# Later activations in the gate pairs, and the index keys' chain and scores behind the operand sums, in a hybrid attention and retention block

## The chip, the cores and the metric

The kernel runs on 1 core of one Trainium2 chip. The time is device microseconds of one execution; a time of the kernel is the median of several. The names in the profile: PE multiplies matrices, PEld loads its weights, DVE and ACT work on vectors (ACT with activation functions), POOL is GpSimd, SP issues DMAs. ACT and POOL issue DMAs as well.

## The reference

One layer over 512 tokens of width 2048. The normed input is multiplied by a wide matrix, whose columns feed a sparse attention (an indexer scores keys, the best 128 are taken), a retention over chunks, and two gates:

```python
h = rmsnorm(x, norm_gain)
proj = h @ w_in
(aq, ak, av, az, iq, ik, iw, rq, rk, rv, rz, ga, gb) = jnp.split(proj, SPLIT_POINTS, axis=-1)
iq = iq.reshape(B, L, IDX_HEADS, IDX_DIM) * (IDX_DIM ** -0.5)
ik = plain_layernorm(ik)
...
a_out = dsa_mixer(aq, ak, av, iq, ik, iw, positions, rel_bias) * jax.nn.silu(az)
b_out = retention_mixer(rq, rk, rv, ret_gn_gain) * jax.nn.silu(rz)
merged = jax.nn.sigmoid(ga) * (a_out @ w_a_out) + jax.nn.sigmoid(gb) * (b_out @ w_b_out)
r = x + merged @ w_o
return r + (p_i @ w_ple) * jax.nn.sigmoid(r @ w_ple_gate)
```

The indexer's score is a sum over 16 heads of `relu(iq . ik) * iw`. A last RMSNorm follows the layer.

## The kernel before

**Numbers as two halves.** Every matrix operand is held as a high and a low 16-bit part, and a product is three matmuls: high by high, high by low, low by high. A unit of weights is a raw tile of 32-bit numbers, loaded by SP (L250), of which ACT makes the high part (`high_part`, L138, tile wh) and DVE the low part (`low_part`, L147, tile wl). The operand hs or hh holds the input's parts.

**Seven products for eight.** Two blocks of 128 output columns are computed as a pair from seven units in place of eight, with sums of weight blocks and of input blocks. `gemm_pair` (L378) runs a pair: fourteen runs of eight blocks of rows, in which a product's first run takes the high part of its unit and the second the low part, into four PSUM banks p, v, q and r. Unit 3 is the first that goes into bank r. After products end, ACT copies banks to SBUF (L389, L413; tiles e, pv) and DVE forms the outputs from them (L396, L400, L1595). For the values, `values_pair` does the same over wider blocks with the weights as the moving side (L1560 to L1562); the sum that it calls t there is a raw tile wt, to which POOL adds a second block by a DMA that accumulates (L237), twice.

**What sets the order.** The program is written out in its final order, with no scheduler: `step()` (L308) is called after each group of matmuls (every two blocks of rows in a pair, so 56 times in a pair), and `later(n, f)` (L302) has f issued n steps later. The engines take their own instructions in the order of issue, so a step number sets what stands ahead of what in an engine's queue. `SPLIT_AT` (L375) says at which run of a pair the parts of a following unit are made: unit 3 in run 2 (PE needs it in run 5), unit 4 in run 4 (its low part in run 8).

**The pairs in question.** `gate_pair` (L1585) serves the merge gates (u_g, 16 pairs), the retention gate (u_rz, 4), queries and keys of the attention (u_qk, 8) and the attention gate (u_az, 4); the 8 pairs of the retention's own queries, keys and values pass `scaled=False` and have no such multiplication. For each of a pair's two outputs, DVE multiplies by the tokens' norm R["b"] (L1599); output 0 is complete after run 11, output 1 after the last. Six steps later `finish` is issued: an activation on ACT (L1606 sigmoid or silu, followed by a store; L1634 silu for the retention, followed by a product and a store on POOL, L1637 and L1638; L1651 for queries and keys, followed 5 or 9 steps later by the low half on DVE, and 4 more steps later by a store from ACT's queue, L1653). Between the pairs ACT also makes masks for the position bias (mk, L1129), which PE multiplies in some pairs.

**The head.** While PE multiplies the index queries and then the retention's values (u_rv), the sums of input blocks that the pairs need are made in eight rounds, by `H_ORDER`: ACT multiplies two blocks by the gain (L1006), DVE makes two sums of them (L618 to L621), then the high and low parts (L601, L145, L147). `NORM_AT` gives the steps of seven functions: `f_sum` and `f_rnat` (the norm), `f_keys1` (transposes, then the index keys' statistics on DVE, L854 to L861, and a power on POOL, L862), `f_bcast` (the norm spread to R["b"]), `f_keys2` (normalised keys, L871), `f_values` (last columns of the values, L878, stored by SP, L884) and `f_keys3` (transposes, and the parts ikh and ikl). From `SCORES_AT` on, 48 scores are issued every third step (matmuls L1030 and L1031, relu on ACT L1035, weighting on DVE L1042 and L1044). Behind them come 48 rounds of a top-k on DVE (L1168 to L1174) at low rate; the rounds not yet run when the pairs start are halved and issued one half at a time inside them (`late_round`, L1580).

Of the kernel before, what the change touches and what calls it, by code (L numbers as in the profile page):

```python
# [16 lines left out]
AF = mybir.ActivationFunctionType  # L17
# [20 lines left out]
class General:  # L38


    fast = False
# [7 lines left out]
class Fast:  # L49


    fast = True
# [12 lines left out]
INDEX_K = 2.0 ** 6  # L65
# [7 lines left out]
def block_kernel(tc, flag, cfg, xT, pT, posb, posq, w_in, w_v, w_r0, w_r1, w_ik, w_a, w_b, w_ad, w_o, w_ple, w_gate,  # L73
                 w_gt, w_pt, fgb, tab, gains, cst, dec, out, out_a, out_b):
    nc = tc.nc
    pe, dve, act, pool, sp = nc.tensor, nc.vector, nc.scalar, nc.gpsimd, nc.sync

    fast = cfg.fast
    un_x, un_a, un_m, un_r, un_p = (1.0 / (cfg.w * v) for v in (cfg.x, cfg.a, cfg.m, cfg.r, cfg.p))

    with contextlib.ExitStack() as ctx:
# [11 lines left out]
        def U(name, dt=F32):  # L93
            return up.tile([128, L], dt, name=name, tag="u")

        def V2(name):
            return vp.tile([128, 2 * L], F16, name=name, tag="v")
# [10 lines left out]
        def P(name):  # L108
            return pp.tile([128, L], F32, name=name, tag="p")

        def pair(t):
            t = t.bitcast(F16)
            return t[:, 0:L], t[:, L:2 * L]
# [4 lines left out]
        def tok(t):  # L118
            return slice(128 * t, 128 * t + 128)
# [11 lines left out]
        def column(n=1, of=0):  # L131
            c = slice(columns[of], columns[of] + n)
            columns[of] += n
            assert columns[of] <= (STATS - HIGHS, STATS)[of]
            return stats[:, c]
# [4 lines left out]
        def low_part(l, src, h, gain=None, checked=False):  # L140

            if not fast:
                h = h.bitcast(F32)
            if gain is None and not (checked and fast):
                dve.tensor_sub(l, src, h)  # L145
            else:
                dve.scalar_tensor_tensor(l, src, 1.0 if gain is None else gain, h, op0=OP.mult, op1=OP.subtract,  # L147
                                         **({"accum_out": column()} if checked and fast else {}))
# [153 lines left out]
        def later(n, f):  # L302
            if n <= 0:
                return f()
            tick[1] += 1
            heapq.heappush(soon, (tick[0] + n, tick[1], f))
# [61 lines left out]
        LO, HI = slice(0, 256), slice(256, 512)  # L368
# [214 lines left out]
        def residual_sums(raw, parts, name="r", gain=cfg.r, nk=8, checked=True):  # L583


            X = {n: [None] * 8 for n in PRODUCTS}
            T = {}

            V_ = {}

            def views(ns, k):
                return V_[ns, k].rearrange("p (j i c) -> p i j c", j=2, i=2)

            def high(ns, k, src, sign):
                if not fast:
                    for j, n in enumerate(ns):
                        t = X[n][k] = U(name + n, F32R)
                        act.activation(t[:, LO], src[:, (LO, HI)[j]], AF.Copy, scale=sign * gain)
                    return
                t = V_[ns, k] = V2(name + ns[0])  # L600
                act.activation(views(ns, k)[:, 0], src.rearrange("p (j c) -> p j c", j=2), AF.Copy, scale=sign * gain)  # L601
                for j, n in enumerate(ns):
                    X[n][k] = t[:, L * j:L * j + L]

            def low(ns, k, src, sign):
                by = None if sign * gain == 1.0 else sign * gain
                if not fast:
                    for j, n in enumerate(ns):
                        low_part(X[n][k][:, HI], src[:, (LO, HI)[j]], X[n][k][:, LO], by, True)
                    return  # L610
                v = views(ns, k)
                low_part(v[:, 1], src.rearrange("p (j c) -> p j c", j=2), v[:, 0], by, checked)

            def one(k, i):
                if i == 0:
                    x, y = raw[k], raw[k + nk]
                    t1, t2 = T[k] = U("t1"), U("t2")
                    dve.tensor_sub(t1[:, LO], x[:, HI], y[:, HI])  # L618
                    dve.tensor_sub(t2[:, LO], x[:, LO], x[:, HI])
                    dve.tensor_sub(t1[:, HI], x[:, LO], t1[:, LO])  # L620
                    dve.tensor_sub(t2[:, HI], y[:, LO], t1[:, HI])  # L621
                    for n, j, q in (("a11", k, LO), ("a12", k + nk, LO), ("a22", k + nk, HI)):
                        X[n][k] = tuple(v[:, q] for v in parts[j])
                else:
                    t1, t2 = T[k] if i < 3 else T.pop(k)
                    for a in ((("s3", "s4"), k, t2, 1.0), (("s1", "s2"), k, t1, -1.0)):
                        (None, None, high, low)[i](*a)

            return X, one
# [83 lines left out]
        hparts = []  # L713
# [25 lines left out]
        def rstd_nat(name, ts=range(NT)):  # L739

            ps = P("ps_ms")
            for t in ts:
                pe.matmul(ps[:, t:t + 1], acc[0][:, tok(t)], ones[:, 0:1], start=True, stop=True)
            r = cp.tile([128, NT], F32, name=name)
            c = slice(ts[0], ts[-1] + 1)
            dve.tensor_scalar(r[:, c], ps[:, c], 1.0 / D, EPS, op0=OP.mult, op1=OP.add)
            pool.tensor_tensor(r[:, c], r[:, c], mhalf[:, c], op=OP.pow)
            return r
# [66 lines left out]
        def f_rnat():  # L815
            R["nat"] = rstd_nat("r_nat")
            acc[0] = acc[1] = None
            later(6 if fast else 0, f_rnat2)

        def f_rnat2():  # L820
            r2w = cp.tile([128, NT], F32, name="r2w")
# [65 lines left out]
        def f_keys3():  # L887
            ps = P("ps_kT")
            for t in range(NT):
                pe.transpose(ps[:, tok(t)], R["kd"][:, tok(t)], ident)  # L890
            if fast:
                ikh, ikl = pair(U("ik"))
                later(2, lambda: act.activation(ikh, ps, AF.Copy, scale=INDEX_K))
                later(4, lambda: low_part(ikl, ps, ikh, INDEX_K, True))
            else:
                ikh = U("ikh", F32R)
                ikl = U("ikl", F32R)
                act.activation(ikh, ps, AF.Copy)
                dve.tensor_sub(ikl, ps, ikh.bitcast(F32))
            R["ik"] = ikh, ikl  # L900
# [102 lines left out]
        if fast:  # L1003
            def gained(k):
                for i in (k, k + 8):
                    act.activation(xs[i], xs[i], AF.Copy, scale=ng[:, i:i + 1])  # L1006

            Xh, h_sums = residual_sums(xs, hparts, "h", 1.0, checked=False)
            for n, k in enumerate(H_ORDER):
                n = H_AT + H_EACH * n  # L1010
                later(n, lambda k=k: gained(k))
                for at, i in H_STEPS:
                    later(n + at, lambda k=k, i=i: h_sums(k, i))
            for n, f in zip(NORM_AT, (f_sum, f_rnat, f_keys1, f_bcast, f_keys2, f_values, f_keys3)):
                later(n, f)
        else:
            todo.extend(N3 * 2 + [f_sum] + N3 * 3 + [f_rnat] + N3 * 3 + [f_bcast, None, f_keys1] + N3 * 3 + [f_keys2] + N3 * 2 + [f_keys3] + N3 + [f_values] + N3)
# [54 lines left out]
        if not fast:  # L1072
            Xh, h_step = combos(lambda k: xn[k], lambda k: xn[k + 8], "h", lambda n, k: x_at.get((n, k)))
# [24 lines left out]
        if fast:  # L1098
            later(SCORES_AT - tick[0], lambda: todo.extend(scores))
        state["rate"] = 1 << 30 if fast else BG_RATES[0]  # L1100
# [484 lines left out]
        def gate_pair(ids, finish, compact=False, scaled=True):  # L1585
            if state["banks"]:
                for n in ROUNDS_AT:
                    later(n, late_round)
            t = B("go")
            outs = [t[:, 0:512], t[:, 512:1024]]  # L1590
            have = [0, 0]

            def done(c0, c1, i, q, f=dve.tensor_add):
                o = outs[i]
                f(o[:, q], c0, c1)  # L1595
                have[i] += 1
                if have[i] == 2:
                    if fast and scaled:
                        dve.tensor_mul(o, o, R["b"])  # L1599
                    later(6 if fast and scaled else 1, lambda: finish(i, o))  # L1600

            gemm_pair(ids, Xh, done, compact=compact and fast, turned=fast)

# [412 lines left out]
        for m in range(MF):  # L2016
            i = u_p[m // 4][0]
# [4 lines left out]
            ps = P("ps_pw")  # L2022
# [285 lines left out]
        for i, c in enumerate((LO, HI)):  # L2308
            for ids, parts, name in ((u_t[0], rparts, "ps_tg"), (u_t[1], pparts, "ps_tw")):
                ps = P(name)  # L2310
# [29 lines left out]
        for q in range(MF // 4):  # L2340
            o = U("yo")
# [8 lines left out]

RV = 488, 488
WIDE, WIDE_LATE = (0, 1, 2, 3, 4, 5, 6), (1, 2, 0, 3, 4, 5, 6)
H_ORDER, H_AT, H_EACH, H_STEPS = (0, 1, 2, 3, 4, 5, 6, 7), 4, 11, ((5, 0), (14, 2), (17, 3))
NORM_AT = 32, 44, 54, 62, 78, 82, 90
SCORES_APART = 2
SCORES_AT = 168
TABLES_AT, TABLE_STEPS = 132, (12, 18, 26, 36, 48, 62)
MF = 12
DONE_AT = (1, 2, 3, 6, 7, 8, 9), (3, 5, 8, 25, 31, 34, 36), (3, 5, 8, 18, 20, 21, 23)
SUM_ORDER = (0, 1, 2, 3, 5, 6, 7, 4)  # L2360
# [149 lines left out]
```

## Time and profile before

| | |
|---|---|
| median of 3 runs | 1563.55 us (1562.85 to 1563.55) |
| profiled execution, its own time | 1562.71 us |
| its span in the profile | 1560.9 us |
| mean granted clock of PE | 0.997 |
| PE busy | 1524.4 us (98%) |
| DVE busy | 1331.5 us (85%) |
| ACT busy | 992.9 us (64%) |
| POOL busy | 241.3 us (15%) |

The span is what the profiler saw, from the first to the last instruction; the time has 1.8 us more around it. A line of a timeline gives the start, the length, the engine, the source line and the operation with the tiles written and read, then the counts of repeats; in brackets stands how long the engine stood idle before it, and what it waited for. Lines of waits give the sum in us, the count and the median. PEclk is the clock that the throttle granted to PE, as a share of full speed.

### The profile page before, as it was taken

The numbers are of one execution on the slowest core, as the hardware profiler recorded it, in microseconds if no ns is written. First come the engines' busy times: TensorE is split into PE (matmuls) and PEld (weight loads), VectorE is DVE, ScalarE is ACT, GpSimd is POOL, SyncE is SP. The second block draws the span as 40 slices with busy tenths as digits, with TensorE's granted clock in tenths as the row PEclk, the third lists the DMA queues.
The fourth block names the chain that finished last, engine by engine and source line by source line (L and its number), as shares of the span: only waits on it lengthen the run. The fifth ranks groups of instructions, "written<-read, shape, count | busy, mean of one in ns | idle before, by whom it ended". The sixth has DMA issues, their size and how long they took to land. (4 is left out here: it accounts for less than half of the span.)

```text
span 1560.9 us, 29786 instructions
## 1 busy us (share of the span) xinstructions
PE 1524.4 (98%) x11321; PEld 1072.0 (69%) x11321; DVE 1331.5 (85%) x2603; ACT 992.9 (64%) x1652; POOL 241.3 (15%) x280
## 2 busy tenths in 40 slices
PE   9989999999999999999999999999999999999997
PEld 5644447988988998996666666755567566647765
DVE  8978768898998998897888887788889999998975
ACT  7856756665566565677776666667754665676654
POOL 3013121111111111113321121200000111101101
PEclk9999999999999999999999999999999999999999
DMA  8489998899899898899988798999687599879973
GB/s 321 131 245 212 291 220 234 224 231 234 214 229 234 224 233 213 230 242 248 256 228 225 200 240 221 255 342 344 227 246 252 145 235 231 237 225 229 267 215 143
DMA packets 137289, 365.74 MB, mean 234 GB/s; under 512 B 22320, under 2 KB 34864, under 8 KB 137136
## 3 DMA queue, kind: packets, MB, share of 16 engines
q1 hardware_dynamic: 92640, 227.89, 42.6%
q0 software_dynamic: 31392, 110.77, 37.9%
q10 hardware_dynamic: 13104, 25.09, 4.3%
q8 instruction: 90, 1.47, 0.4%
q14 instruction: 63, 0.52, 0.1%
HBM read 319.13 MB, written 42.99 MB: 232 GB/s over the span
## 5 line engine op out<-in xcount | busy, mean ns | idle before, releaser
L147 DVE SCALAR_TENSOR_TENSOR wl<-wraw,wh 128x1024 f16<-128x1024 f32 (+2 forms) x464 | 560.5, 1216 | 127.7 <-ACT wh L138 121.6
L462 PEld LDWEIGHTS <-wh 128*128 128x128 f16 x5096 | 496.7, 98 | 187.9 <-ACT wh L138 18.9
L138 ACT ACTIVATE wh<-wraw 128x1024 f16<-128x1024 f32 (+2 forms) x487 | 495.5, 1025 | 151.9 <-DVE wraw L285 74.2
L462 PEld LDWEIGHTS <-wl 128*128 128x128 f16 x3024 | 294.2, 98 | 45.8 <-DVE wl L147 2.3
L237 POOL DMA_DIRECT2D wraw<-w_in x120 | 106.6, 964 | 586.6 <-DVE wl L147 528.6
L462 PE MATMUL ps_p<-hs,wh 128*128 128x256 f16 (+1 forms) x1024 | 153.5, 299 | 0.0
L389 ACT ACTIVATE e<-ps_p 128x256 f32<-128x256 f32 (+1 forms) x147 | 70.4, 479 | 89.5 <-PE ps_p L462 82.4
L462 PE MATMUL ps_r<-hs,wh 128*128 128x256 f16 (+1 forms) x512 | 76.2, 299 | 14.8 <-ACT wh L138 14.7
L462 PE MATMUL ps_p<-hs,wl 128*128 128x256 f16 x640 | 84.3, 273 | 0.4 <-DVE wl L147 0.3
L462 PE MATMUL ps_q<-hh,wh 128*128 128x256 f16 x640 | 76.5, 273 | 0.0
L462 PE MATMUL ps_v<-hh,wh 128*128 128x256 f16 x640 | 76.4, 273 | 0.0
L462 PE MATMUL ps_p<-hh,wh 128*128 128x256 f16 x640 | 76.4, 273 | 0.0
L462 PE MATMUL ps_v<-hs,wh 128*128 128x256 f16 (+1 forms) x512 | 76.1, 299 | 0.0
L1129 ACT ACTIVATE mk<-relf,thr 128x512 f16<-128x512 f32 (+3 forms) x128 | 68.6, 555 | 4.8 <-DVE qk L147 3.1
L285 DVE TENSOR_TENSOR wraw<-wraw 128x1024 f32<-128x1024 f32 x54 | 66.1, 1225 | 1.9
L1606 ACT ACTIVATE go<-go 128x512 f32<-128x512 f32 x40 | 25.2, 630 | 61.6 <-DVE go L1599 61.6
L356 PEld LDWEIGHTS <-wl 128*128 128x128 f16 x364 | 35.6, 98 | 37.1 <-issue 0.8
L354 PEld LDWEIGHTS <-wh 128*128 128x128 f16 x364 | 35.7, 98 | 33.4 <-DVE z L154 0.7
L355 PEld LDWEIGHTS <-wh 128*128 128x128 f16 x364 | 35.6, 98 | 32.5
L355 PE MATMUL ps_w<-bh,wh 128*128 128x512 f16 x128 | 48.5, 379 | 0.5 <-DVE bh L147 0.5
L354 PE MATMUL ps_w<-bh,wh 128*128 128x512 f16 x128 | 48.5, 379 | 0.0
L356 PE MATMUL ps_w<-bh,wl 128*128 128x512 f16 x128 | 48.5, 379 | 0.0
(508 smaller groups left out, 2863.8 us busy)
## 6 DMA issues: line engine op xcount, KB each, us to landing
wraw<-w_in SPq DMA_DIRECT2D x170, 512.0 KB, 5.3
wraw<-w_in POOLq DMA_DIRECT2D x120, 512.0 KB, 7.8
wraw<-w_o SPq DMA_DIRECT2D x32, 512.0 KB, 5.4
wraw<-w_o POOLq DMA_DIRECT2D x24, 512.0 KB, 7.5
wraw<-w_gate SPq DMA_DIRECT2D x24, 512.0 KB, 5.6
wraw<-w_v SPq DMA_DIRECT2D x16, 512.0 KB, 7.9
wraw<-w_b SPq DMA_DIRECT2D x16, 512.0 KB, 6.2
wraw<-w_r SPq DMA_DIRECT2D x16, 488.0 KB, 5.6
```

The costliest lines, as they stand in the source:

```text
L138: act.activation(h, src, AF.Copy, scale=by, **({"accum_out": column(1, 1)} if summed else {}))
L147: dve.scalar_tensor_tensor(l, src, 1.0 if gain is None else gain, h, op0=OP.mult, op1=OP.subtract, **({"accum_out": column()} if checked a ...
L237: pool.dma_start(out=view(raw_tiles[r], nk, cols), in_=src[:, k0:k0 + nk, :], accum_op=OP.add)
L285: dve.tensor_add(raw, raw, view(raw_tiles[plus], nk, cols))
L354: pe.matmul(o, h[:, k, w], a, start=(s == order[0]), stop=False)
L355: pe.matmul(o, h[:, k, w], b, start=False, stop=False)
L356: pe.matmul(o, l[:, k, w], a, start=False, stop=(s == order[-1]))
L389: act.activation(E[n][:, cs], src[:, cs], AF.Copy)
L462: pe.matmul(o[:, co], w[:, k], src, start=(n < 4 and begin and k == 0 and j == 0), stop=(ended[n] == 2 * nk), skip_group_check=True)
L1129: act.activation(bias_e[b][i // per][:, ln * (i % per):ln * (i % per + 1)], relf[:, :ln], AF.Sign, bias=thr[:, q:q + 1])
L1606: act.activation(o, o, func, scale=un_x)
```

## The change

Nothing is computed in another way: instructions change places. In all 32 scaled gate pairs the activation, with what follows it, is issued 12 steps behind the multiplication in place of 6. In the head, the sums of input blocks go through the blocks in another order; the norm's steps, the broadcast, the keys' three functions and the values' last columns are issued later (`NORM_AT`), by 4 to 46 steps each; the scores start 38 steps later, and the tables of positions 18. The operands that are parts of the input itself (a11, a12, a22) are entered all at once, ahead of the rounds.

```diff
         def f_rnat():
...
-            later(6 if fast else 0, f_rnat2)
+            later(36 if fast else 0, f_rnat2)
...
                 ikh, ikl = pair(U("ik"))
-                later(2, lambda: act.activation(ikh, ps, AF.Copy, scale=INDEX_K))
-                later(4, lambda: low_part(ikl, ps, ikh, INDEX_K, True))
+                later(5, lambda: act.activation(ikh, ps, AF.Copy, scale=INDEX_K))
+                later(9, lambda: low_part(ikl, ps, ikh, INDEX_K, True))
...
             Xh, h_sums = residual_sums(xs, hparts, "h", 1.0, checked=False)
+            for k in range(8):
+                for n, j, q in (("a11", k, LO), ("a12", k + 8, LO), ("a22", k + 8, HI)):
+                    Xh[n][k] = tuple(v[:, q] for v in hparts[j])
...
                     if fast and scaled:
                         dve.tensor_mul(o, o, R["b"])
-                    later(6 if fast and scaled else 1, lambda: finish(i, o))
+                    later(FINISH if fast and scaled else 1, lambda: finish(i, o))
...
-H_ORDER, H_AT, H_EACH, H_STEPS = (0, 1, 2, 3, 4, 5, 6, 7), 4, 11, ((5, 0), (14, 2), (17, 3))
-NORM_AT = 32, 44, 54, 62, 78, 82, 90
+H_ORDER, H_AT, H_EACH, H_STEPS = (2, 3, 4, 5, 6, 7, 0, 1), 4, 11, ((5, 0), (14, 2), (17, 3))
+NORM_AT = 36, 54, 100, 94, 116, 124, 128
 SCORES_APART = 2
-SCORES_AT = 168
-TABLES_AT, TABLE_STEPS = 132, (12, 18, 26, 36, 48, 62)
+FINISH = 12
+SCORES_AT = 206
+TABLES_AT, TABLE_STEPS = 150, (12, 18, 26, 36, 48, 62)
```

The steps of `NORM_AT` belong, in this order, to f_sum, f_rnat, f_keys1, f_bcast, f_keys2, f_values and f_keys3. The lines of the changed kernel are numbered 3 higher behind that loop.

Three places show what moves. First, ACT's queue at the start of a pair of queries and keys: qk is the activation's output (two of them, one for each output of the pair before), wh a unit's high part, mk2 a mask, e3, pv and e1 copies of banks. Before:

```order
L1129 ACTIVATE mk2_11290<-relf_527,thr_528 128x256
L1651 ACTIVATE qk_11296<-go_11086 128x512
L389 ACTIVATE e3_11302<-ps_p_11087 128x512
L138 ACTIVATE wh_11316<-wraw_11160 128x1024
L1129 ACTIVATE mk2_11290<-relf_527,thr_528 128x256
L1651 ACTIVATE qk_11341<-go_11086 128x512
L1653 DMA qd_1044<-qk_11296 128x512
L1129 ACTIVATE mk2_11290<-relf_527,thr_528 128x256
L138 ACTIVATE wh_11353<-wraw_11192 128x1024
L389 ACTIVATE pv_11366<-ps_v_11313 128x512
```

In the changed order the same place reads:

```order
L389 ACTIVATE e3_11288<-ps_p_11074 128x512
L138 ACTIVATE wh_11302<-wraw_11148 128x1024
L1132 ACTIVATE mk2_11278<-relf_527,thr_528 128x256
L1654 ACTIVATE qk_11318<-go_11073 128x512
L1132 ACTIVATE mk2_11278<-relf_527,thr_528 128x256
L138 ACTIVATE wh_11337<-wraw_11180 128x1024
L1654 ACTIVATE qk_11351<-go_11073 128x512
L389 ACTIVATE pv_11353<-ps_v_11299 128x512
L1656 DMA qd_981<-qk_11318 128x512
L1132 ACTIVATE mk2_11278<-relf_527,thr_528 128x256
L413 ACTIVATE e1_11366<-ps_p_11298 128x256
L138 ACTIVATE wh_11368<-wraw_11081 128x1024
```

The second wh of each excerpt is the high part of unit 3: it stood behind the second qk and the first store, and now stands ahead of both. The wh that ends the second excerpt is that of unit 4, now the first high part behind them.

Second, SP's loads in the head: wt are the four tiles that POOL adds to, rd<-rvx the store of the values' last columns. Before:

```order
L250 DMA wraw_1052<-w_r0 128x976
L250 DMA wt_1081<-w_r1 128x976
L884 DMA rd_531<-rvx_1063 128x4x24 x2
L250 DMA wt_1109<-w_r1 128x976
L250 DMA wt_1134<-w_r1 128x976
```

And now:

```order
L250 DMA wt_1069<-w_r1 128x976
L250 DMA wt_1102<-w_r1 128x976
L250 DMA wraw_1249<-w_r1 128x976
L250 DMA wraw_1268<-w_r1 128x976
L250 DMA wraw_1292<-w_r1 128x976
L250 DMA wraw_1321<-w_r1 128x976
L884 DMA rd_531<-rvx_1284 128x4x24 x2
```

The store stood between the first and the second of the four tiles; it now stands behind the fourth and four more loads.

Third, POOL's accumulating DMAs in the head, each tile with a first and a second one. Before:

```order
L862 TENSOR_TENSOR krs_900<-krs_900,mhalf_95 128x4
L237 DMA wt_1081<-w_r1 128x976
L237 DMA wt_1109<-w_r1 128x976
L237 DMA wt_1134<-w_r1 128x976
L237 DMA wt_1081<-w_r0 128x976
L237 DMA wt_1164<-w_r1 128x976
```

And now:

```order
L237 DMA wt_1013<-w_r1 128x976
L237 DMA wt_1039<-w_r1 128x976
L237 DMA wt_1069<-w_r1 128x976
L862 TENSOR_TENSOR krs_1178<-krs_1178,mhalf_95 128x4
L237 DMA wt_1013<-w_r0 128x976
L237 DMA wt_1102<-w_r1 128x976
```

The index keys' power (krs) went behind the first three; the fourth tile's first addition (the last row) stands in both behind the first tile's second one.

## The prediction

> **What bounds the kernel now.** I read the page's share of busy time first, then the waits of PE, then the busy time by stretch, then the timelines around one wait.
>
> ```profile
> span 1560.9 us, 29786 instructions
> PE 1524.4 (98%) x11321; PEld 1072.0 (69%) x11321; DVE 1331.5 (85%) x2603; ACT 992.9 (64%) x1652; POOL 241.3 (15%) x280
> ```
>
> PE is the bound: 36.5 us of the span are all that an order can win. The profiled execution took 1562.71 us, 1.8 us more than its span; the median of the runs is 1563.55, 0.8 above it. I sum against 1562.7.
>
> The waits of PE, as sum in us, count and median:
>
> ```profile
> PE ps_r L462 <- ACT wh L138: 14.7, 11, 2.7
> PE ps_vp L1561 <- DVE wl L147: 2.8, 2, 1.9
> PE ps_vv L1560 <- ACT wh L138: 2.6, 1, 2.6
> ```
>
> The largest is one place in a pair of output blocks: the bank r's first matmuls, which need the high part of the pair's unit 3. By stretch (length, then PE, PEld, DVE, ACT and POOL busy, granted clock, DMA share, GB/s):
>
> ```profile
> 706.99:1027.20 320.21, 304.99 (x2435) 216.57 (x2433) 259.96 (x455) 221.80 (x350) 74.97 (x95) 1.00 0.90 238
> 60.00:100.00 40.00, 37.60 (x220) 21.63 (x218) 38.14 (x108) 27.82 (x46) 4.88 (x5) 1.00 0.57 172
> 100.00:140.00 40.00, 36.56 (x177) 17.68 (x176) 24.73 (x54) 21.87 (x35) 12.03 (x14) 0.96 0.99 221
> 180.00:220.00 40.00, 38.99 (x186) 18.01 (x185) 31.73 (x62) 26.81 (x40) 5.31 (x6) 1.00 0.90 233
> ...
> 767.17:788.17 21.00, 18.43 (x138) 13.15 (x137) 17.27 (x28) 14.26 (x22) 6.78 (x8) 1.00 0.88 239
> 890.98:912.07 21.09, 18.43 (x137) 13.22 (x136) 17.02 (x32) 12.72 (x20) 2.77 (x4) 1.00 0.82 211
> ```
>
> The sixteen pairs of the retention gate, the queries and keys and the attention gate (706.99 to 1027.20) lose 320.21 - 304.99 = **15.2 us**; the head loses 2.4, 3.4 and 1.0 us in its three stretches, and at a mean clock of 0.96 some 40 x 0.04 = 1.6 more: **8.4 us**. Both are places that the change touches. A third stretch says where it can win nothing, the retention and merge gate pairs:
>
> ```profile
> 300.00:600.00 300.00, 300.00 (x2853) 270.13 (x2851) 271.39 (x589) 177.32 (x257) 48.87 (x54) 1.00 0.89 225
> ```
>
> One pair, of queries and keys, shows the cause. T0 = 890.98 is its first matmul. PE, then ACT, then DVE:
>
> ```profile
> 890.98 1.89 PE L462 MATMUL ps_v<-hs,wh 128*128 128x512 f16 x8
> 896.20 1.91 PE L462 MATMUL ps_q<-hh,wh 128*128 128x256 f16 x16
> 900.77 1.90 PE L462 MATMUL ps_r<-hs,wh 128*128 128x512 f16 x8 [2.66 <-ACT wh L138]
> 904.25 0.93 PE L462 MATMUL ps_p<-hs,wl 128*128 128x256 f16 x7
> ```
>
> ```profile
> 892.96 0.63 ACT L1651 ACTIVATE qk<-go 128x512 f16<-128x512 f32 x1 [2.55 <-DVE go L1599]
> 897.08 0.63 ACT L1651 ACTIVATE qk<-go 128x512 f16<-128x512 f32 x1 [1.66 <-DVE go L1599]
> 898.89 0.33 ACTq L1653 DMA_DIRECT2D qd<-qk  x1
> 899.26 0.51 ACT L1129 ACTIVATE mk<-relf,thr 128x256 f16<-128x256 f32 x1 [1.55 <-DVE qk L147]
> 899.67 1.04 ACT L138 ACTIVATE wh<-wraw 128x1024 f16<-128x1024 f32 x1
> ...
> 901.50 0.37 ACT L413 ACTIVATE e<-ps_p 128x256 f32<-128x256 f32 x1
> 901.76 1.05 ACT L138 ACTIVATE wh<-wraw 128x1024 f16<-128x1024 f32 x1
> ```
>
> ```profile
> 896.35 0.69 DVE L1599 TENSOR_TENSOR go<-go,r_b 128x512 f32<-128x512 f32 x1
> ...
> 898.10 0.69 DVE L147 SCALAR_TENSOR_TENSOR qk<-go,qk 128x512 f16<-128x512 f32 x1
> ```
>
> DVE multiplies output 1 of the pair before at 896.35; ACT waits 1.66 for it, then 1.55 more for the low half that its own DMA issue needs; only then, at 899.67, comes the high part of unit 3. Eight-matmul runs of PE follow each other at 1.72 to 1.75, so r was due at 896.20 + 1.75 = 897.95 (T0+7.0) and began 2.8 later. ACT has time; it stands in its queue. The group of these waits over the sixteen pairs:
>
> ```profile
> ACT qk L1651 <- DVE go L1599: 30.2, 16, 2.5
> ACT go L1634 <- DVE go L1599: 15.7, 6, 3.2
> ACT go L1606 <- DVE go L1599: 15.0, 8, 2.6
> ```
>
> **The change: activations 12 steps behind.** A pair is 56 steps, so a step is 18.43/56 = 0.33 us and an activation is issued 2 us later in the order. Output 1's now stands behind the high part of unit 3, which then runs when its raw weights and buffers allow: output 0's activation goes from T0+2.0 on, the high part some 1.6 to 2.5 later, at T0+3.6 to 4.5, against the T0+7.0 at which it is due. The 15.2 us lose their cause.
>
> What is late next: the high part of unit 4, on ACT behind output 1's activation, and its low part on DVE. PE uses the low part in the run that began at 904.25, without the stall at 904.25 - 2.8 - 890.98 = T0+10.45. From the end of the multiplication (897.04) the chain is, by the rows above, 1.75 to the end of the low half (898.79), 0.47 for the DMA issue (to 899.26), 0.41 for a mask (to 899.67), 0.26 for the copy of bank p (901.50 to 901.76), 1.05 for the high part and 1.22 for the low part (8.5 us for seven, by a row below): 5.2 us. The multiplication ended at T0+6.06, so this pair would be late by 0.8. In the rz pairs there is no such DMA on ACT's queue, but the multiplication ends latest there, before this row:
>
> ```profile
> 774.73 0.63 ACT L1634 ACTIVATE go<-go 128x512 f32<-128x512 f32 x1 [3.20 <-DVE go L1599]
> ```
>
> That is T0+7.5 (767.17), and without the low half and the DMA the chain is about 0.5 + 0.5 (activation and copy) + 0.41 + 0.26 + 1.05 + 1.22 = 4.0: 1.1 late. Five pairs, from this one to the one at 890.98, have a multiplication behind T0+5.3 and no matmuls of a bias tile between; with a bias tile a pair has more cover:
>
> ```profile
> 912.07:932.30 20.23, 20.23 (x201) 14.84 (x200) 16.77 (x30) 14.27 (x24) 7.15 (x12) 1.00 0.95 246
> ```
>
> Its PE work is 1.8 longer than 18.43, and those matmuls lie ahead of unit 4's low part. So 1.1 + 4 x 0.8 = 4.3 us stay. Three more of these pairs carry half a top-k round on DVE (more rounds are left for them, since scores come later), which may push a multiplication: 0.4 more. Gain: 15.2 - 4.3 - 0.4 = **10.5 us**, between 5 (a wait of 1.0 in each of the ten pairs without a bias tile) and 15.2.
>
> The 32 activations of the merge gates move likewise and gain nothing: PE is busy 300.00 of 300.00 us there. If that cover fails (a unit 4 late there), each pair would lose what it does here, 0.8; nothing in the row hints at it, with ACT busy 177 of 300. The stores behind the moved activations (POOL's, ACT's) leave 2 us later each; their readers are later stages, the last of them 60 us of az pairs behind the last query. I cost that at nothing.
>
> **The change: the head.** Moved out of the stretch in which DVE is full (38.14 of 40 us): the keys' statistics with the broadcast's start, and the normalised keys, by these two windows (DVE is the third pair of numbers):
>
> ```profile
> 72.23:75.40 3.17, 2.70 (x17) 1.43 (x16) 2.96 (x19) 3.02 (x5) 0.13 (x1) 1.00 0.53 158
> 84.20:86.06 1.86, 1.86 (x11) 0.89 (x10) 1.86 (x9) 1.85 (x7) 0.01 (x1) 1.00 0.17 69
> ```
>
> That is 2.96 + 1.86 = 4.8 us of DVE, more than the 2.4 that PE waits there (for low parts, L1561): they go. SP's queue changes too:
>
> ```profile
> 80.92 0.43 SPq L250 DMA_DIRECT2D wt<-w_r  x1
> 85.62 0.94 SPq L884 DMA_DIRECT2D rd<-rvx  x2
> ```
>
> The store of the values' last columns, which waited until 85.62, no longer stands ahead of three of the four t tiles; they can start some 5 us earlier. Yet the wait at 113 to 116 has another end:
>
> ```profile
> 101.61 0.89 POOL L237 DMA_DIRECT2D wt<-w_r  x1 [5.45 <-DVE isc L1042]
> 102.85 0.88 POOL L237 DMA_DIRECT2D wt<-w_r  x1 [0.35 <-DMA wt<-w_r]
> ```
>
> ```profile
> 115.13 1.02 ACT L138 ACTIVATE wh<-wt 128x976 f16<-128x976 f32 x1 [5.69 <-DMA wt<-w_r]
> ```
>
> ```profile
> DMA to landing us min/median/max: 4.8/8.0/12.2
> ```
>
> The fourth tile's first addition stands behind the first tile's second on POOL, in both orders, and that one needs the first tile's low part. In the new order it is: high part 1.02, the keys' statistics 2.96 (now ahead of that low part), low part 1.17 (as 976 of 1024 columns of 1.22), two issues of 0.9, and a landing of 8.0: 14.9, against the 5 units of some 2.5 us and the transposes between that PE has in hand, about 13.5. Left: 1.4 and 1.0 for the high part, a little less than now; then the first score, whose operand's low half is now behind the last t tile's low part, 1.2 + 0.6 = 1.8; 1.0 at 180:220; and 1.0 of clock. Sum 6.2 against 8.4: gain **2.2**. Bounds: with landings of 4.8 nothing waits at the tile, and the gain is about 7; with 12.2 the tile waits 4.2 longer and the head loses 2 to 3.
>
> On that landing the Trainium skill (DMA: Bandwidth & Descriptors, Anatomy of one DMA — SWDGE (gpsimd) path) fits 2.0 us plus the bytes by 436e3 per us; for 128 x 976 x 4 bytes that estimate is 3.1 us, and by it the wait at the tile would be gone. The row disagrees: no landing here was under 4.8.
>
> The clock in that stretch:
>
> ```profile
> 115.00:120.00 5.00, 2.95 (x8) 1.11 (x8) 3.78 (x7) 4.08 (x6) 1.36 (x2) 0.73 1.08 226
> ```
>
> PE waited long enough there to lose clock, while waits of 2.6 us in the pairs left it at 1.00. So no clock term enters for the pairs. The Trainium skill (TensorE: Matmul & The Clock Gate, Part 1: The HAM clock gate) halves the clock after an idle window of about 3.4 us that runs free; both rows agree with it.
>
> **Rivals.** *Short landings*: the t tiles' transfers start earlier, in a stretch with a DMA share of 0.57, not 0.99, and take nearer 4.8; the head gains 7: 1562.7 - 10.5 - 7 = 1545. Against it: more of them are then in flight together. *The wait moves to unit 4*: DVE is busy 17.0 to 17.3 us of a pair of 18.43, so with PE's waits gone its multiplications may slip against T0; 1.0 us in ten pairs leaves a gain of 5: 1562.7 - 5 - 2.2 = 1555.5. *The head loses*: landings of 12.2: 1562.7 - 10.5 + 3 = 1555. *It does nothing*: the pairs are held by DVE's throughput with its own waits, and keep their length: 1563 within 3 us. *Slower*: DVE cannot run ahead, because it too waits for ACT's high parts (3.3 us in one pair):
>
> ```profile
> L147 DVE SCALAR_TENSOR_TENSOR wl<-wraw,wh 128x1024 f16<-128x1024 f32 x7 | 8.5, 1222 | 3.3 <-ACT wh L138 3.3
> ```
>
> If output 1's activation, still waiting at its new place, holds unit 4 in all pairs as it now holds unit 3 in the worst, all sixteen are as long as the longest, 21.09: 16 x 21.09 - 320.2 = 17.2 more, less 2.2 of the head: 1577.7. It decides when the pairs' mean length passes 320.21/16 + 2.2/16 = 20.15. Against it: five pairs of sixteen only have a multiplication that late.
>
> **How the numbers follow.** Forecast (both gains, 1545.5 to 1553.5): 1562.7 - 10.5 - 2.2 = **1550**, chance 0.50. Short landings 0.14, unit 4 0.13, the head loses 0.08, nothing 0.07, slower 0.08. A measurement of this kernel can tell 0.2%, 3.1 us, from no change. Faster: 0.50 + 0.14 + 0.13 + 0.08 = 0.85; same 0.07; slower 0.08. The range takes in the first four: from 1541.5 (15.2 in the pairs and 6 in the head) to 1558 (under 5 in the pairs and nothing in the head).
>
> **What would show it.** Right: PE's wait of bank r for the high part falls from 14.7 to under 2; ACT's waits for the multiplication stay, without PE behind them; what PE waits for in the pairs is bank p with a low part, some 4 us, in the pairs without a bias tile; the pairs together take about 310; no PE wait between 60 and 100, and one of 2 us at the fourth t tile. Wrong: pairs of 20 us and more with waits for a low part of DVE (then the slip of the multiplications was underrated), a longer wait between 100 and 125 or before the first score, or a new wait in the gate pairs between 250 and 700.

## The result, and the profile after

| | median | runs | ratio to before (95%) |
|---|---|---|---|
| before | 1563.55 us | 1562.85 to 1563.55 (3) | |
| changed | 1552.33 us | 1550.55 to 1552.77 (3) | 0.9927 (0.9904 to 0.9949) |

The change is faster by 11.2 us, 0.7%, where 13.5 (1563.55 to 1550) was forecast. The profiled execution took 1552.33 us, with a span of 1550.5: 10.4 less than that of before, from which the forecast took 12.7. The waits of PE in the changed kernel stand below as sum in us, count and longest wait. The third number is the longest in the earlier lines of waits too, where I called it the median; no sum used it.

```profile
PE ps_v L462 <- ACT wh L138: 7.5, 6, 1.7
PE ps_vp L1564 <- DVE wl L147: 1.8, 3, 0.9
...
PE ps_vv L1563 <- ACT wh L138: 1.5, 1, 1.5
PE ps_vv L1564 <- DVE wl L147: 0.9, 1, 0.9
PE ps_p L462 <- DVE wl L147: 0.7, 2, 0.5
```

The wait of bank r, 14.7 us before, is gone. In its place bank v waits 7.5 us for unit 5's high part, which was not forecast. By stretch, with the columns as before: the sixteen pairs, the pair at the same place as the one quoted in the prediction, and the head.

```profile
704.56:1017.20 312.64, 304.34 (x2435) 216.73 (x2433) 264.91 (x464) 222.46 (x351) 74.69 (x95) 1.00 0.90 241
881.23:901.38 20.15, 18.61 (x138) 13.08 (x137) 16.58 (x33) 12.61 (x20) 2.62 (x4) 1.00 0.82 214
60.00:100.00 40.00, 39.83 (x229) 22.53 (x227) 37.11 (x101) 27.20 (x40) 6.25 (x5) 1.00 0.68 201
100.00:140.00 40.00, 37.62 (x182) 18.17 (x181) 24.07 (x54) 20.76 (x32) 13.21 (x16) 0.96 1.01 225
140.00:180.00 40.00, 38.71 (x192) 18.57 (x190) 31.66 (x64) 24.38 (x38) 7.21 (x8) 1.00 1.05 293
```

The sixteen pairs take 312.6 us in place of 320.2: **7.6** gained, 10.5 forecast. They start at 704.56 in place of 706.99: **2.4** gained in the head, 2.2 forecast. What lies behind the pairs took 533.3 in place of 533.7. These are single executions: over the experiments below, the start scatters by up to 1 us among kernels with the same head (704.5 to 705.5 in five with the new one, 707.0 to 708.0 in three with the old one, whose means are 2.6 apart), and the part behind the pairs took 531.7 to 534.8 us without a change there.

ACT's queue in the pair at 881.23 shows the old wait gone and the new one:

```profile
884.19 1.05 ACT L138 ACTIVATE wh<-wraw 128x1024 f16<-128x1024 f32 x1
886.86 0.63 ACT L1654 ACTIVATE qk<-go 128x512 f16<-128x512 f32 x1 [1.63 <-DVE go L1602]
...
894.26 0.33 ACTq L1656 DMA_DIRECT2D kd<-qk  x1
894.64 0.51 ACT L1132 ACTIVATE mk<-relf,thr 128x256 f16<-128x256 f32 x1 [3.53 <-DVE go L1598]
895.05 1.04 ACT L138 ACTIVATE wh<-wraw 128x1024 f16<-128x1024 f32 x1
```

Unit 3's high part is done at 885.24 (T0+4.0, as forecast), and ACT's wait of 1.63 for the multiplication has nothing close behind it that PE needs: unit 4's low part, made from the next high part, comes 0.20 late. Then ACT stands 3.5 us ahead of the issue of the second store, kd. The profile names the DVE instruction that ended last, but the store needs the second output's low half (output 1's, as qd and kd are the stores of outputs 0 and 1), and DVE does that late:

```profile
892.01 1.23 DVE L285 TENSOR_TENSOR wraw<-wraw 128x1024 f32<-128x1024 f32 x1
893.16 0.42 DVE L1171 MAX8 m<-isc 128x8 f32<-128x256 f32 x1
893.49 0.68 DVE L147 SCALAR_TENSOR_TENSOR qk<-go,qk 128x512 f16<-128x512 f32 x1
```

It ends at 894.17, the store is issued at 894.26, the high part behind it starts at 895.05. PE runs through bank r without a wait, and now waits for that one:

```profile
888.20 1.89 PE L462 MATMUL ps_r<-hs,wh 128*128 128x512 f16 x8
...
896.15 1.05 PE L462 MATMUL ps_v<-hh,wh 128*128 128x256 f16 x8 [1.33 <-ACT wh L138]
```

So my theory after the result was: in the pairs, the second store's issue in ACT's queue is the remaining bound, not DVE's throughput; in the head, what remains is the index keys' statistics and their power on POOL, not the landing of the transfers. Rivals: DVE's throughput (16.6 us of work in the pair of 20.15) for the one, landing for the other, and that the two parts of the change don't simply add.

### The profile page after: what moved, and what is told of

Same layout as the page of the kernel before. It is cut to its first block, busy times and chain, and to the rows that moved or that the text cites. A ratio compares the mean times of both kernels' runs of the same rounds, so it can differ in the third digit from the quotient of the medians.

```text
span 1550.5 us, 29821 instructions
## 1 busy us (share of the span) xinstructions
PE 1524.0 (98%) x11321; PEld 1072.3 (69%) x11321; DVE 1332.5 (86%) x2603; ACT 990.8 (64%) x1652; POOL 242.5 (16%) x280
## 5 line engine op out<-in xcount | busy, mean ns | idle before, releaser
L237 POOL DMA_DIRECT2D wraw<-w_o x24 | 21.1, 945 | 177.2 <-DVE wl L147 136.5
```

The source lines that it names most:

```text
L237: pool.dma_start(out=view(raw_tiles[r], nk, cols), in_=src[:, k0:k0 + nk, :], accum_op=OP.add)
```

## The experiments

In the tables of this part "pairs" is the length of the sixteen pairs in that kernel's profiled execution, "start" the time at which they begin. Each median stands beside the one of before that was measured on the same chip with it; start and pairs of before are those of its profile.

**The two parts apart.** The first kernel keeps the distance of 12 and puts the head's tables and lags back (the operands entered all at once stay); the second keeps the head and has

```diff
-FINISH = 12
+FINISH = 6
```

> Only the activations go 12 steps behind; the head is as before. If the two parts of the change add up, the time is that of before less what the sixteen pairs gained between the two profiles (320.2 to about 312.6 us): 1563.5 - 7.6 = 1556, and PE's wait of bank v for a high part stands at about 7.5 us. If the head's order is what made room in the pairs (through top-k rounds left for them), the pairs lose more or less than that by over 2 us.

> Only the head is changed; activations stay 6 steps behind. If the parts add up: the first of the sixteen pairs starts 2.4 us earlier and the pairs stay at 320 us, or up to 1 longer for the three more pairs with a half round of top-k: 1561 to 1562. If the head's gain was a by-product of the activations: 1563.5, no change.

| | median | ratio (95%) | start | pairs |
|---|---|---|---|---|
| before | 1563.60 us | | 706.99 | 320.2 |
| activations only | 1552.01 us | 0.9927 (0.9913 to 0.9941) | 707.98 | 310.6 |
| head only | 1563.76 us | 1.0005 (0.9996 to 1.0014) | 704.66 | 321.7 |

The activations alone make the whole gain; the head alone makes none. Both expectations failed by 2 to 4 us: the head starts the pairs 2.3 us earlier, but with the head's change the pairs are longer, by 1.5 us (321.7 against 320.2) and by 2.0 (312.6 against 310.6). Of the 4 us by which the activations alone beat their expectation, these 2.0 are the part that the pairs show; the part behind the pairs was 1.7 shorter and the start 1.0 later than in the profile of before, and why is open. The pairs of the two kernels, first the activations only:

```profile
707.98:1018.57 310.59, 303.88 (x2435) 216.86 (x2433) 263.45 (x459) 223.99 (x353) 74.86 (x95) 1.00 0.92 244
```

```profile
704.66:1026.37 321.71, 304.99 (x2435) 216.51 (x2433) 262.97 (x464) 221.58 (x350) 74.81 (x95) 1.00 0.91 238
```

DVE's top-k maxima (L1171) count 9 in the pairs of the one and 12 in the other, and so do the replacements that follow them (L1175). The scores come 38 steps later, so one round of the top-k instead of four is done ahead of the gate pairs, and three more pairs of queries and keys carry a round each, in two halves; the prediction and the expectations speak of half a round. PE's waits in the pairs follow. With the activations alone bank v waits 5.4 us, where 7.5 was expected, and with the head alone bank r waits 16.2 in place of 14.7:

```profile
PE ps_v L462 <- ACT wh L138: 5.4, 4, 1.7
```

```profile
PE ps_r L462 <- ACT wh L138: 16.2, 11, 2.6
```

**Where the head's gain went.** Both kernels that follow issue the early rounds at a higher rate, so that four are done there as before; one on the head alone, one on the changed kernel.

```diff
-BG_RATES = (2, 12, 40, 7, 6)
+BG_RATES = (2, 4, 40, 7, 6)
```

> The head's change alone (activations 6 steps behind), and the top-k rounds ahead of the gate pairs issued every 4th step in place of every 12th, so that four of them are done there as before the change and none of the three more half rounds is left for pairs of queries and keys. If those half rounds are what gives the head's 2.4 us back: 1563.7 - 2.4 = 1561.3, with the pairs at 320 us. If something else in the later stages gives it back: 1563.7, as with the head alone.

> The changed kernel with the same earlier top-k rounds. If three half rounds in three late pairs cost the 2.0 us by which these pairs are longer here than with the activations alone (312.6 against 310.6): 1552.3 - 2 = 1550.3, and bank v's wait for a high part falls from 7.5 to about 5.4. If not: 1552.

| | median | ratio (95%) | start | pairs |
|---|---|---|---|---|
| before | 1563.03 us | | 706.99 | 320.2 |
| head, rounds earlier | 1561.69 us | 0.9990 (0.9981 to 0.9999) | 705.31 | 321.9 |
| changed, rounds earlier | 1549.64 us | 0.9916 (0.9903 to 0.9930) | 705.43 | 310.6 |

Both came out within 0.7 us of the expectation: the rounds give 2.1 us to the head alone (1563.76 to 1561.69) and 2.7 to the changed kernel. Each taken against the before beside it, as the chips differ, it is 1.5 and 2.2; the head with the rounds earlier is then worth 1.3 us in all, with an interval of 0.2 to 3.0, and the expected 2.4 lies within it without being shown. In the changed one the pairs show it, and bank v waits 5.4 us, as expected:

```profile
705.43:1015.98 310.55, 303.86 (x2435) 216.72 (x2433) 263.01 (x459) 223.63 (x353) 74.70 (x95) 1.00 0.92 246
```

That is the length with the activations only, and again 9 maxima. In the profiled execution of the head alone the pairs are not shorter, though:

```profile
705.31:1027.17 321.86, 306.68 (x2435) 217.13 (x2433) 260.09 (x455) 222.04 (x350) 74.80 (x95) 0.99 0.90 237
```

PE is busy 306.68 here and 304.99 in the row of the head alone; the clock of 0.99 says why, and a stretch of 5 us shows the place (below, on the hardware). Without those 1.7 us it is 320.2, and PE's wait of bank r is 14.7 again.

**The second store.** The changed kernel, with both stores later in the one and only the second in the other:

```diff
-                    later(QK_LOW[i] + 4, lambda: act.dma_start((qd, kd)[i][h], t))
+                    later(QK_LOW[i] + 8, lambda: act.dma_start((qd, kd)[i][h], t))
```

```diff
+                    later(QK_LOW[i] + (4, 8)[i], lambda: act.dma_start((qd, kd)[i][h], t))
```

> The changed kernel with the stores of queries and keys issued 8 steps behind their low half in place of 4, each behind one more high part in ACT's queue. If ACT's wait for DVE's second low half, at the issue of that store, is what holds the high part that bank v needs: that wait of PE falls from 7.5 to under 1.5 us and the time from 1552.3 to 1546. If the pairs are held by DVE's throughput (17 us of work in 18.4), PE waits for DVE in its place and the time stays at 1551 or over.

> The changed kernel with only the second store of a pair (kd) issued 4 steps later, the first left in place. If ACT's wait at the second store holds the high part for bank v, and its wait at the first store the smaller waits of bank p one run of eight earlier (1.6 us in all, by matmul starts): 1552.3 - 8 = 1544.3, 1.5 above both stores later (1542.7). If the first store is the one that counts: 1550 or over.

| | median | before beside it | ratio (95%) | pairs |
|---|---|---|---|---|
| both stores later | 1542.73 us | 1563.60 us | 0.9869 (0.9854 to 0.9884) | 302.9 |
| second store later | 1542.86 us | 1562.94 us | 0.9873 (0.9858 to 0.9888) | 303.6 |

The store is the cause, and DVE's throughput is not: the pairs' waits vanish, and the time is 3.3 us better than the 1546 expected. The pairs are 9.8 shorter: 8.2 are the waits of banks v and p, and PE's own busy time is 1.7 less (304.34 to 302.68).

```profile
705.33:1008.18 302.85, 302.68 (x2435) 217.90 (x2433) 265.35 (x468) 224.23 (x353) 74.88 (x95) 1.00 0.94 251
877.12:895.38 18.26, 18.26 (x138) 13.31 (x137) 16.39 (x33) 12.84 (x20) 2.62 (x3) 1.00 0.92 233
```

The sixteen pairs are 0.2 us longer than PE is busy, and in a single pair DVE does the same 16.4 us of work in 18.26 us. The high part and the store have changed places on ACT:

```profile
886.75 1.06 ACT L138 ACTIVATE wh<-wraw 128x1024 f16<-128x1024 f32 x1 [1.85 <-DVE wraw L285]
887.67 0.33 ACTq L1656 DMA_DIRECT2D kd<-qk  x1
```

The second store alone does it, 1.4 us better than expected: the small waits of bank p, which I had put down to the first store, went too, without its being moved. The likely way, not tried by itself, is that what ACT lost at the second store of one pair made the next pair's units late.

**The first store in the order of before.** The same edit of both stores, in the kernel before, with activations at 6 steps.

> The kernel before, activations at 6 steps, with both stores 4 steps later, so that unit 3's high part stands behind the second activation but no longer behind the first store. In the pair of the prediction ACT waited 1.66 for the multiplication and 1.55 for the low half. If both waits made up the delay of unit 3, the eight pairs that carry such stores win up to 1.55 each, 8.7 by their single waits: 1563.3 - 8.7 = 1554.6, and some 6 us stay, which only the distance of the activation takes. If the multiplication alone set it: 1563.

It took 1555.62 us (before 1562.94; 0.9953, 0.9939 to 0.9966), pairs 311.8: 7.3 gained of the 8.7 expected, and of the wait of bank r this stays:

```profile
PE ps_r L462 <- ACT wh L138: 5.2, 4, 2.6
```

The pairs alone are 8.4 us shorter in the profile, near the 8.7. They hold a loss that the profile of before does not have: the wait of 2.57 us that stays in one pair of the retention gate cost PE some of its clock (0.72, and 0.94 in the next 5 us):

```profile
775.00:780.00 5.00, 2.68 (x7) 1.03 (x8) 3.03 (x6) 4.82 (x9) 2.12 (x2) 0.72 0.96 215
```

So 7.3 of the 11.6 us that the distance gains by itself (1563.60 to 1552.01) come with a later store as well; the 5.2 us left are those in which unit 3 still stands behind the wait for the multiplication, and they are gone with the distance.

**The gate pairs.** The changed kernel, with the sixteen merge gate pairs back at six steps:

```diff
-                    later(FINISH if fast and scaled else 1, lambda: finish(i, o))
+                    later((FINISH if state["banks"] else 6) if fast and scaled else 1, lambda: finish(i, o))
```

> The changed kernel with the activations of the sixteen merge gate pairs back at 6 steps, the other sixteen at 12. If the gate pairs gain nothing from the distance, since PE waits for nothing there either way: 1552.3. If it matters there, the time goes up by more than 3.

1551.59 us (before 1563.03; 0.9929, 0.9916 to 0.9943): no difference from the changed kernel's 1552.33 beyond the spread of its runs (1550.55 to 1552.77). A cost or gain of the distance there is not to be seen; PE is busy 300.00 us between 300 and 600 in both.

**The index keys on POOL.** In the changed kernel, POOL and ACT around the four tiles:

```profile
98.51 1.90 POOL L862 TENSOR_TENSOR krs<-krs,mhalf 128x4 f32<-128x4 f32 x1 [12.53 <-DVE krs L861]
100.38 2.71 POOL L237 DMA_DIRECT2D wt<-w_r  x3
```

```profile
108.76 1.92 ACT L138 ACTIVATE wh<-wt 128x976 f16<-128x976 f32 x2 [5.63 <-DMA wt<-w_r]
```

```profile
DMA to landing us min/median/max: 4.4/8.8/13.0
```

The power takes 1.9 us and stands ahead of three additions, one of them the fourth tile's first. The edit puts the statistics 6 steps later:

```diff
-NORM_AT = 36, 54, 100, 94, 116, 124, 128
+NORM_AT = 36, 54, 106, 94, 116, 124, 128
```

> The changed kernel with the index keys' statistics 6 steps later, so that their power stands behind the fourth tile's first addition in POOL's queue and their 2.9 us on DVE behind the first tile's low part. If that power and those statistics set the wait at the fourth tile: the additions are issued some 2 us earlier, the waits of 1.5 and 0.9 us and the dip of the clock (0.66 for 5 us, 1.7) go: 1552.3 - 2.4 to - 4 = 1548 to 1550. If the transfers' landing sets it (5 to 13 us, sharing the DMA engines), it stays: 1552.

It took 1549.20 us (0.9908, 0.9893 to 0.9923), 3.1 less than the changed kernel, as expected if the power and the statistics set the wait. POOL, and then the two stretches of 5 us in which PE had waited and lost clock:

```profile
98.95 1.78 POOL L237 DMA_DIRECT2D wt<-w_r  x2 [12.36 <-DVE wl L147]
...
104.58 1.04 POOL L862 TENSOR_TENSOR krs<-krs,mhalf 128x4 f32<-128x4 f32 x1 [1.87 <-DVE krs L861]
```

```profile
105.00:110.00 5.00, 4.56 (x21) 1.95 (x20) 4.29 (x13) 3.13 (x5) 1.55 (x2) 1.00 1.03 231
110.00:115.00 5.00, 4.54 (x24) 2.42 (x24) 2.68 (x6) 3.79 (x9) 2.30 (x3) 1.00 1.08 195
```

The additions of the first tile and of the fourth go out at 98.95 and just after, 1.4 us earlier. The landings are no shorter (median 8.8 in both). PE still waits 0.9 us (4.56 and 4.54 of 5), but the clock stays at 1.00. In the changed kernel those rows are

```profile
105.00:110.00 5.00, 3.47 (x18) 1.56 (x16) 0.19 (x1) 1.24 (x2) 0.86 (x1) 1.00 1.05 235
110.00:115.00 5.00, 4.15 (x14) 1.60 (x13) 3.28 (x6) 3.02 (x7) 2.08 (x3) 0.66 1.10 208
```

So the 3.1 us are, to 0.1, the wait of 1.5 and a clock loss of 0.34 x 5 = 1.7. The edit moves the statistics and the power together, and no run tells them apart. The timelines of the first tile's high and low part do, in part; the changed kernel first, then this one:

```profile
95.99 1.02 ACT L138 ACTIVATE wh<-wt 128x976 f16<-128x976 f32 x1 [0.66 <-PE ps_vq L1565]
98.34 1.17 DVE L147 SCALAR_TENSOR_TENSOR wl<-wt,wh 128x976 f16<-128x976 f32 x1
```

```profile
96.36 1.02 ACT L138 ACTIVATE wh<-wt 128x976 f16<-128x976 f32 x1 [0.66 <-PE ps_vq L1565]
97.40 1.18 DVE L147 SCALAR_TENSOR_TENSOR wl<-wt,wh 128x976 f16<-128x976 f32 x1 [1.17 <-ACT wh L138]
```

Behind the high part, the statistics held the low part for 1.3 us (97.01 to 98.34), which is 0.0 with the edit. From the end of the low part to the first addition it took 0.9 (99.51 to 100.38), against 0.4 (98.58 to 98.95): some 0.5 us for the power. By these rows the statistics on DVE are the larger share.

**All together.** Later stores, later keys and earlier rounds.

> The changed kernel with the stores later, the index keys' statistics 6 steps later and the earlier rounds together. The first two gained 9.6 and 3.1 us. If they are separate places, and the rounds' 2 us lie within the 9.6 (a pair without that wait has room for them): 1552.3 - 9.6 - 3.1 = 1539.6; if the rounds add as well: 1537.6; if DVE's throughput becomes the bound: 1542 or over.

1539.64 us (before 1563.03; 0.9852, 0.9837 to 0.9867), the sum of the two larger parts to 0.1 us by the medians; with each kernel taken against the before beside it, the sum is 0.7 short (23.4 gained, of 11.2 + 9.7 + 3.2). Either way the rounds' 2 us do not come on top: the pairs are as long with three rounds fewer as with later stores alone (302.73 and 302.85).

```profile
702.84:1005.57 302.73, 302.63 (x2435) 217.90 (x2433) 263.07 (x459) 224.47 (x353) 74.70 (x95) 1.00 0.94 252
...
100.00:140.00 40.00, 39.09 (x196) 19.21 (x195) 28.45 (x72) 22.74 (x35) 13.50 (x16) 1.00 1.04 232
```

This beats both kernels. Its pairs hold 0.1 us of waits.

## Why the prediction was right, and where it was not

**Right: the cause and the size of the main term.** The place (unit 3's high part, behind the activation and the first store in ACT's queue) and the time at which it would now be done, T0+3.6 to 4.5, hold: T0+4.0. By the experiment on the kernel before, the 14.7 us were made of both waits quoted: 9.5 go with the store's place, 5.2 only with the distance. ACT's waits for the multiplication did not stay, as I had said, but fell from 60.9 to 24.7 us in the pairs.

**Wrong: "what is late next".** The prediction followed the queue to unit 4 and priced its low part at 4.3 us. Bank p waits 0.7. I counted the first store and stopped; the second store is issued 12 steps behind the first, waits for a low half that in the pair shown stands on DVE behind a sum (1.23 us) and a top-k instruction (0.42), and it holds the next high part: ACT stood 1.2 to 3.9 us at each of the eight second stores, and PE 7.5 us behind them. In the kernel before, the second store had found its low half done, and ACT stood 0.2 us:

```profile
902.67 0.33 ACTq L1653 DMA_DIRECT2D kd<-qk  x1
903.04 0.91 ACT L1129 ACTIVATE mk<-relf,thr 128x256 f16<-128x256 f32 x2 [0.23 <-ACT wh L138]
```

The pairs' gain came only 3 us short because two errors went against each other, which is luck: 4.3 priced where 0.7 came, and nothing priced where 7.5 came.

**Under-sized: the top-k rounds.** Three more pairs with rounds were priced at 0.4, as half a round each, and cost 2.0 in the changed kernel (312.6 against 310.6, and 310.6 again with the rounds earlier); each carries both halves of one. With them the head's change, forecast at 2.2 and measured at 2.4 in its own stretch, shows no gain as a whole.

**Right in sum by luck, not in its parts: the head.** The waits from 60 to 100 went (39.83 of 40 us busy, 37.60 before), with all of the head's changes together; which of them did it was not tried. At the fourth tile 1.5 and 0.9 us are left where 1.4 and 1.0 were forecast, by a chain that had the statistics on DVE, but not the power on POOL behind them. The 1.8 us forecast for the first score did not come: it is multiplied at 122.71 without a wait. PE's loss between 140 and 220 is 1.8 us, where 1.0 was forecast to stay, and is at low parts of a later pair of values, the first of them here:

```profile
122.71 0.27 PE L1033 MATMUL ps_is<-ik,taz 128*128 128x256 f16 x1
...
174.20 0.38 PE L1564 MATMUL ps_vp<-wl,hh 128*128 128x512 f16 x1 [0.89 <-DVE wl L147]
```

The clock lost 1.7 where 1.0 was forecast.

**The rivals.** "The wait moves to unit 4" was near in kind, and its reason, multiplications that slip against T0, was wrong in the pair looked at: the second one ended at T0+5.60 (886.14 + 0.69 - 881.23) where it had ended at T0+6.06. "Slower", by the same reason, fails with it: with the stores later DVE fits its work in 18.26 us. Landings were not shorter (median 8.8, 8.0 before).

## What to carry to other kernels

A store issued from a compute engine's queue waits there for its data, and everything behind it waits too (here up to 3.9 us): place it behind the last instruction that the bound engine needs soon. When an order is moved, follow every wait of the moved step to the end of its chain, the second one as well as the first. Work that is put off in one stage is done in another: see what that one has room for before the first stage's gain is booked.

## What the runs showed of the hardware

The clock. I said that no clock term enters for the pairs, since waits of 2.6 us had left PE at 1.00. The same wait, at the same place, did lose the clock in other executions. In the head with earlier rounds:

```profile
900.00:905.00 5.00, 5.00 (x29) 3.29 (x28) 3.87 (x9) 3.29 (x6) 0.00 (x0) 0.66 0.82 233
```

In before, the same pair, which waited as long (2.66 us), shows

```profile
900.00:905.00 5.00, 4.23 (x31) 3.04 (x32) 3.97 (x7) 3.72 (x7) 0.00 (x0) 1.00 0.87 222
```

A loss of 0.34 over 5 us is 1.7 us, as PE's busy time in that kernel's pairs was 1.7 longer. The wait of 2.57 in the kernel before with later stores lost the clock too (the row of 0.72 above), and did not in before. So a wait of 2.6 us loses the clock in some executions and not in others. In the head the waits of 2.6 and 0.9 close together (before) and of 1.5 and 0.9 close together (changed) both lost it, in the profiled executions; 0.9 in all did not.

That a loss comes and goes fits a window that runs free of the program, as the Trainium skill has it (TensorE: Matmul & The Clock Gate, Part 1: The HAM clock gate). The idle window of about 3.4 us that the same section of the Trainium skill gives does not fit: none of these waits was longer than 2.7, and I was wrong to say that both rows agree with it. How much of a window must be idle, no run here shows.
